# Three numbers that set the order of a mixer's instructions: the block inverse and the spatial gate are placed earlier

## The chip, the cores and the metric

The kernel runs on one NeuronCore of a Trainium2 chip. The time is that of the device in microseconds (us), from the start of the program to its end on that core. Engines are called as in the profile: PE (TensorE), DVE (VectorE), ACT (ScalarE), POOL (GpSimd) and SP (SyncE, which here only issues transfers).

## The reference

One encoder layer over S = 1024 frames of D = 1024 channels, in float32. What matters here:

```python
x = layer_norm(x)
proj = x @ w_in                               # u, v, r, k, val, wd, ad, gd, two gates
y_a = gelu(u) * (w_s @ layer_norm(gelu(v)) + b_s)      # spatial gate, blocks of 128 frames
for t in frames:                              # RWKV7: 16 heads of 64 channels
    sa    = state @ (-kk[t])
    state = state * w[t] + outer(sa, kk[t] * a[t]) + outer(v[t], k[t])
    y[t]  = state @ r[t]
y_b = (group_norm(y) + bonus) * g
m = sigmoid(gate_a) * y_a + sigmoid(gate_b) * y_b
x = layer_norm(alpha * x + m @ w_o)
x = layer_norm(alpha * x + conv_ffn(x))
```

## The kernel before

**Three parts.** The head makes the first layer norm and the spatial gate's normed v. The mixer makes everything up to the layer norm after w_o. The convolutional FFN ends the program. All wide products are of 128x512 with both operands split into two parts of reduced precision, so that one product takes three matmuls (`xh,wh`, `xlo,wh`, `xh,wl`, into `ps`). ACT casts a weight block to `wh`, and POOL subtracts to make `wl<-wr,wh`.

**Units.** The mixer's recurrence runs over 16 units: unit u is half h = u % 2 (512 frames, 8 chunks of 64) of the pair of heads p = u // 2. Each unit has four stages, named by letters in `run` (L1018):

- A, `stage_a` (L639), prepares unit u+2 while unit u runs: decays `gams`, normed keys (with a round trip through memory, SP's `q_d<-f`, `rc<-q_d`, `q_d<-rc`, `f<-q_d`), the products `ar<-tkr,gams` and `f<-f` on POOL, `bd<-f` and `ar<-f,gams` on DVE, the score products `pp<-ar,bd` on PE, which DVE masks into `ny<-pp,tri` and `ar<-pp,tri`; then four transfers `a_d<-ny` put 32x32 blocks to memory.
- B, `stage_b` (L732), inverts the triangular blocks of unit u+1: four transfers `bd<-a_d` bring them in one block to a partition; DVE copies `ydx<-rowm`; POOL runs 31 pairs of `tm<-ydx,bd` and `ydx<-ydx,tm`, each waiting for the one before; DVE transposes (`ydx<-ydx`, then four times `ny<-ydx`); PE multiplies `pp<-ydx,ny` and `pp<-ny,ydx`, with ACT copies between.
- C, `stage_chain` (L772), is the sequential pass over the 8 chunks (`pc`, `py`, `xs`, `bs`, `sgm`), which needs the inverse of its unit.
- F, `stage_fin`, ends a unit.

Around them stand the spatial gate Z (`stage_z`, L861: a small product with the mask, `bsb`, `fs<-pp,par,bsb` on DVE, two `gu<-gu,fs` on POOL) and the wide products U, W, X, k, r, v, which are only work to fill PE.

Buffers: `bd`, `ydx`, `tm` exist once; `ar`, `bs`, `ny` and the memory block `a_d` twice, by half. In the instruction lists `ar_1476`, `ny_1480`, `a_d_69` belong to even units and `ar_1477`, `ny_1481`, `a_d_70` to odd ones; `q_d_65` and `q_d_67` serve the norms of even units, `q_d_66` and `q_d_68` those of odd ones.

**What sets the order.** All instructions of the mixer are recorded by a class `Weave` first, with their dependencies and a modelled cost. `order` (L218) then lays them out by list scheduling over five queues (PE, DVE, ACT, POOL, SP): it takes the queue that can start something earliest, and of the instructions that can start there the one with the smallest `(o.prio, o.seq)` (L237). Its result is emitted as it stands (L279), so each engine runs a fixed list, and an instruction whose operand is late holds up all that follow it on its engine. `at(u, cls, ...)` (L999) gives a stage its priority, 100 * u + cls; with cls None the PE instructions go last of all (10^6 and up) and the others get 100 * u + 3. The whole mixer therefore shows as L279 in the profile, and the head and the FFN as L92.

Of the kernel before, what the change touches and what calls it, by code (L numbers as in the profile page):

```python
# [283 lines left out]
def hybrid_block(ctx: ExitStack, tc, x, w_in, w_v, pars, rows, bs, ws, lor, w_o, w_up, w_dn, out):  # L284
    nc = tc.nc
    W = Weave(tc)
# [296 lines left out]
    with ExitStack() as st:  # L583
# [415 lines left out]
        def at(u, cls, fn, *args):  # L999
            tick[0] += 1  # L1000
            n = 10 ** 6 + tick[0]
            W.prio = (lambda key: n if key == "T" else 100 * u + 3) if cls is None else 100 * u + cls
            W.cls = fn.__name__
            return fn(*args)
# [13 lines left out]
        def run(ch, u):  # L1018
            p, h = divmod(u, 2)
            if ch == "C":  # L1020
                at(u, 0, stage_chain, p, h)
            elif ch == "B" and u + 1 < NU:
                at(u, 10, stage_b, *divmod(u + 1, 2))
            elif ch == "A" and u + 2 < NU:
                at(u, 8, stage_a, *divmod(u + 2, 2))
            elif ch == "F":
                at(u, 5, stage_fin, p, h)
            elif ch == "v" and p + 1 < NPAIR:
                at(u, None, stage_g, p + 1, "v")
            elif ch in "kr" and p + 2 < NPAIR:  # L1030
                at(u, None, stage_g, p + 2, ch)
            elif ch in "UWZX":
                q = done[ch]
                if q < NPAIR - (ch in "XW") and (q < done["X"] + 1 and q < p + 1
                                                 if ch != "X" else ("yb", q, 1) in gen):
                    done[ch] += 1
                    at(u, 30 if ch == "Z" else None, {"U": stage_u, "W": stage_ga, "Z": stage_z, "X": stage_gb}[ch], q)

        done = dict.fromkeys("UWZX", 0)
        for u in range(NU - 1):  # L1040
            for ch in {0: "CFvUBAZW", 1: "CFBArXkW", NU - 3: "CFBAZW", NU - 2: "XUCFBZ"}.get(
                    u, "CFBAZWkr" if u % 2 else "XCFvUBA"):
                run(ch, u)
        u = NU - 1
# [196 lines left out]
```

## Time and profile before

| | |
|---|---|
| time, median of 3 runs (lowest to highest) | 1964.5 us (1964.23 to 1970.06) |
| time of the profiled execution | 1965.61 us |
| its span, first to last instruction | 1963.8 us |
| granted clock of TensorE, mean | 0.982 |
| PE busy | 1854.9 us, 94% |
| PE weight load (PEld) busy | 1499.5 us, 76% |
| DVE, ACT, POOL busy | 994.2, 857.2, 916.0 us |

PE is busy nearly all the time; PEld is the loading of weights into the array, which overlaps PE. A busy share is a mean over the head, the mixer (whose last wide product on PE starts at 1264.00 us) and the FFN.

### The profile page before, as it was taken

To read this page: it belongs to the slowest core of one execution; us is meant where nothing else is said; L and a number is where in the kernel's file an instruction comes from. 1 tells how busy PE (TensorE), PEld (TensorE's weight loads), DVE (VectorE), ACT (ScalarE), POOL (GpSimd) and SP (SyncE) were. 2 spreads that over 40 slices of the span, in tenths; PEclk is the share of its full clock that TensorE was granted. 3 is DMA by queue.
4 is the path that set the end of the run, shared out by engine and by line. 5 is a ranking of instruction groups with operands and counts; after the bars stand their busy time and mean duration, and the time that the engine had idled before them with its cause. 6 is when DMAs were issued, how large, how long until landed. Compare 5 with 4: busy or idle time off the path is not lost.

```text
span 1963.8 us, 27242 instructions
## 1 busy us (share of the span) xinstructions
PE 1854.9 (94%) x10024; PEld 1499.5 (76%) x10024; DVE 994.2 (51%) x1806; ACT 857.2 (44%) x1733; POOL 916.0 (47%) x1505
## 2 busy tenths in 40 slices
PE   6997899999999999999998899989999999999997
PEld 5996677677777777777776677768888888888886
DVE  8423745666555567555554467683333332333327
ACT  5544465655556566556565565421212121212121
POOL 5202575557656565675548662272423232323224
PEclk9998999999999999999998999999999999999999
DMA  6112121111112122112131322231111111111102
GB/s 211 33 49 61 46 64 58 52 46 47 55 52 68 55 54 63 38 58 65 47 93 55 97 86 62 79 115 44 54 43 55 42 55 42 57 41 58 39 1 86
DMA packets 78884, 119.13 MB, mean 61 GB/s; under 512 B 27776, under 2 KB 47488, under 8 KB 78752
## 3 DMA queue, kind: packets, MB, share of 16 engines
q1 hardware_dynamic: 60640, 96.94, 16.3%
q10 hardware_dynamic: 18112, 20.45, 3.2%
q8 instruction: 80, 1.31, 0.3%
q14 instruction: 52, 0.43, 0.1%
HBM read 103.08 MB, written 14.29 MB: 60 GB/s over the span
## 4 chain that ended last, share of the span: by engine, by line
PE 64%; POOL 17%; DVE 9%; issue 4%; ACT 3%; DMA 2%; ACTq 1%; POOLq 0%; SPq 0%; DVEq 0%
PE ps L279 17%; PE ps L92 11%; PE pu L92 11%; PE pd L92 10%; PE pp L279 8%; POOL ydx L279 6%; POOL tm L279 6%; PE pv L92 4%; PE pc L279 2%; POOL wl L279 2%; POOL ar L279 1%; PE py L279 1%; DVE ln_st L92 1%; DVE vl L92 1%; DVE f L92 1%
## 5 line engine op out<-in xcount | busy, mean ns | idle before, releaser
L279 PE MATMUL ps<-xh,wh 128*128 128x512 f32 x896 | 373.4, 417 | 33.2 <-DVE tkr L279 13.1
L279 PE MATMUL ps<-xh,wl 128*128 128x512 f32 x896 | 369.2, 413 | 6.6 <-POOL wl L279 6.3
L279 PE MATMUL ps<-xlo,wh 128*128 128x512 f32 x896 | 373.3, 417 | 0.0
L279 PEld LDWEIGHTS ps<-xh,wh 128*128 128x128 f32 x896 | 173.4, 194 | 66.3 <-DVE tkr L279 14.6
L279 PEld LDWEIGHTS ps<-xh,wl 128*128 128x128 f32 x896 | 173.0, 193 | 37.3 <-POOL wl L279 8.3
L279 POOL TENSOR_TENSOR tm<-ydx,bd 128x60 f32<-128x60 f32 (+24 forms) x496 | 167.3, 337 | 67.4 <-DMA bd<-a_d 12.4
L279 PEld LDWEIGHTS ps<-xlo,wh 128*128 128x128 f32 x896 | 173.2, 193 | 29.0 <-issue 1.0
L279 POOL TENSOR_TENSOR wl<-wr,wh 128x1024 fp32r<-128x1024 f32 x50 | 122.3, 2445 | 149.7 <-ACT wh L279 130.3
L92 DVE SCALAR_TENSOR_TENSOR t<-gb,par,t 128x512 f32<-128x512 f32 x84 | 89.6, 1067 | 193.4 <-ACT t L92 192.0
L279 POOL TENSOR_TENSOR ydx<-ydx,tm 128x60 f32<-128x60 f32 (+24 forms) x496 | 167.0, 337 | 37.2
L279 DVE SCALAR_TENSOR_TENSOR bs<-pc,gams,sgm 64x64 f32<-64x64 f32 x240 | 67.9, 283 | 161.5 <-PE pc L279 159.2
L92 POOL TENSOR_TENSOR fdl<-wr,fdh 128x1024 fp32r<-128x1024 f32 x21 | 51.4, 2463 | 196.4 <-ACT fdh L92 196.4
L92 PE MATMUL pd<-fdh,th 128*128 128x512 f32 x336 | 130.7, 389 | 0.0
L92 PE MATMUL pd<-fdl,th 128*128 128x512 f32 x336 | 130.7, 389 | 0.0
L92 PE MATMUL pd<-fdh,tl 128*128 128x512 f32 x336 | 130.7, 389 | 0.0
L92 ACT CAST fdh<-wr 128x1024 fp32r<-128x1024 f32 x21 | 21.5, 1051 | 196.5 <-PE pd L92 182.7
L92 POOL TENSOR_TENSOR wl<-wr,wh 128x1024 fp32r<-128x1024 f32 x22 | 56.3, 2560 | 63.6 <-ACT wh L92 63.6
L92 POOL TENSOR_TENSOR ful<-wr,fuh 128x1024 fp32r<-128x1024 f32 x20 | 48.7, 2437 | 78.7 <-ACT fuh L92 72.9
L279 PEld LDWEIGHTS pp<-ar,bd 64*128 64x128 f32 x512 | 61.8, 189 | 27.6 <-issue 17.8
L279 ACT ACTIVATE sgm<-bs,gams 128x128 f32<-128x128 f32 x128 | 51.4, 401 | 71.1 <-DVE bs L279 67.6
L92 POOL TENSOR_TENSOR tl<-t,th 128x512 fp32r<-128x512 f32 x42 | 55.6, 1325 | 56.2 <-DVE th L92 56.2
L279 PE MATMUL pp<-ar,bd 64*128 64x128 f32 x512 | 74.8, 288 | 6.1 <-DVE ar L279 4.7
(356 smaller groups left out, 4460.8 us busy)
## 6 DMA issues: line engine op xcount, KB each, us to landing
wr<-in_dram SPq DMA_DIRECT2D x113, 512.0 KB
bd<-a_d SPq DMA_DIRECT2D x64, 128.0 KB
vraw<-in_dram SPq DMA_DIRECT2D x8, 528.0 KB
xt<-in_dram SPq DMA_DIRECT2D x8, 512.0 KB
v_d<-xt ACTq DMA_DIRECT2D x8, 512.0 KB
fv<-v_d ACTq DMA_DIRECT2D x16, 256.0 KB
f<-q_d SPq DMA_DIRECT2D x32, 128.0 KB
m_d<-gu ACTq DMA_DIRECT2D x14, 256.0 KB
```

Source lines behind the costliest of these rows:

```text
L92: return fn(*a, **k)
L279: fn(*a, **k)
```

## The change

Two of the numbers in `run` change. B's class goes from 10 to 6, so that at one u the inverse of unit u+1 stands ahead of A, the preparation of unit u+2 (8). Z's goes from 30 to 4, ahead of F (5), B and A and behind the chain C (0) and the work of the wide products on engines other than PE (3). No instruction is added, removed or altered in shape; the five queues of the mixer get another order.

```diff
             if ch == "C":
                 at(u, 0, stage_chain, p, h)
             elif ch == "B" and u + 1 < NU:
-                at(u, 10, stage_b, *divmod(u + 1, 2))
+                at(u, 6, stage_b, *divmod(u + 1, 2))
             elif ch == "A" and u + 2 < NU:
                 at(u, 8, stage_a, *divmod(u + 2, 2))
             elif ch == "F":
...
-                    at(u, 30 if ch == "Z" else None, {"U": stage_u, "W": stage_ga, "Z": stage_z, "X": stage_gb}[ch], q)
+                    at(u, 4 if ch == "Z" else None, {"U": stage_u, "W": stage_ga, "Z": stage_z, "X": stage_gb}[ch], q)
```

On POOL, at the end of the inverse of unit 7 (the pairs of `tm` and `ydx`), there stood before:

```order
L279 TENSOR_TENSOR tm<-ydx,bd 128x35
L279 TENSOR_TENSOR ydx<-ydx,tm 128x7x5
L279 TENSOR_TENSOR ar_1476<-tkr,gams 64x8x64 x2
L279 TENSOR_TENSOR tm<-ydx,bd 128x28
L279 TENSOR_TENSOR ydx<-ydx,tm 128x7x4
...
L279 TENSOR_TENSOR tm<-ydx,bd 128x8
L279 TENSOR_TENSOR ydx<-ydx,tm 128x8
```

Of the change, the same place on POOL reads:

```order
L279 TENSOR_TENSOR tm<-ydx,bd 128x28
L279 TENSOR_TENSOR ydx<-ydx,tm 128x7x4
...
L279 TENSOR_TENSOR tm<-ydx,bd 128x8
L279 TENSOR_TENSOR ydx<-ydx,tm 128x8
L279 TENSOR_TENSOR ar_1476<-tkr,gams 64x8x64 x2
```

The two products `ar` of the preparation of unit 8 left the inverse and follow it.

On PE, at the end of the inverse of unit 6, before, the score products of unit 7 (`ar_1477,bd`) stood ahead of the product that takes up the inverse of unit 6 (`ydx,ny_1480`):

```order
L279 MATMUL pp<-ar_1477,bd 128x128 x4
L279 MATMUL ps<-xh_119,wh 128x512
L279 MATMUL pp<-ident,bd 128x128 x4
...
L279 MATMUL pp<-cm,tv 128x128 x3
L279 MATMUL pp<-f,bones 128x512
...
L279 MATMUL pp<-ydx,ny_1480 32x32 x16
L279 MATMUL ps<-xh_119,wh 128x512
```

Of the change they stand behind it:

```order
L279 MATMUL pp<-ident,ff 128x128 x4
L279 MATMUL pp<-gd_136,g0w 128x512
L279 MATMUL pp<-gd_137,g1w 128x512
L279 MATMUL pp<-ydx,ny_1480 32x32 x16
L279 MATMUL pp<-ar_1477,bd 128x128
L279 MATMUL ps<-xh_119,wh 128x512
L279 MATMUL pp<-ar_1477,bd 128x128 x3
L279 MATMUL pp<-ny_1480,ydx 32x32
```

The preparation of the next unit and the end of the inverse changed places.

On SP, the four loads `bd<-a_d_70` of unit 7 and the round trip of the norms of unit 8 (`q_d_65`, `rc`, `q_d_67`), before:

```order
L279 DMA a_d_70<-ny_1481 32x8x32 x2
L279 DMA bd<-a_d_70 32x1024 x2
L279 DMA q_d_65<-f 1x512
L279 DMA lraw<-in_dram 128x384
L279 DMA bd<-a_d_70 32x1024
L279 DMA q_d_65<-f 1x512
L279 DMA rc<-q_d_65 128x8
L279 DMA bd<-a_d_70 32x1024
L279 DMA wr<-in_dram 128x1024
L279 DMA q_d_67<-rc 128x8
L279 DMA f<-q_d_67 64x512 x2
```

Of the change:

```order
L279 DMA a_d_70<-ny_1481 32x8x32
L279 DMA q_d_65<-f 1x512
L279 DMA bd<-a_d_70 32x1024
L279 DMA rc<-q_d_65 128x8
L279 DMA bd<-a_d_70 32x1024
L279 DMA q_d_67<-rc 128x8
L279 DMA wr<-in_dram 128x1024
L279 DMA bd<-a_d_70 32x1024
L279 DMA f<-q_d_67 64x512 x2
L279 DMA bd<-a_d_70 32x1024
```

The fourth load, without which the inverse can't start, moved behind the whole round trip of the next unit's norms.

## Rows read from the trace of the kernel before

**Rows 1.** The page: busy time of each engine, share of the span, instructions.

```profile
PE 1854.9 (94%) x10024; PEld 1499.5 (76%) x10024; DVE 994.2 (51%) x1806; ACT 857.2 (44%) x1733; POOL 916.0 (47%) x1505
```

**Rows 2.** The page: the chain that ended last, share of the span by engine.

```profile
PE 64%; POOL 17%; DVE 9%; issue 4%; ACT 3%; DMA 2%; ACTq 1%; POOLq 0%; SPq 0%; DVEq 0%
```

**Rows 3.** Windows, inverse 2 to 14: us, busy PE PEld DVE ACT POOL, clock, DMA.

```profile
602.20:712.50 110.30, 108.92 (x699) 84.07 (x700) 67.00 (x143) 67.92 (x158) 73.52 (x154) 1.00 0.19 56
...
952.50:1091.30 138.80, 125.55 (x756) 97.62 (x752) 70.11 (x146) 77.23 (x167) 82.15 (x158) 0.96 0.25 78
sum 724.50, PE 690.50 PEld 535.92 DVE 415.08 ACT 425.05 POOL 440.67; mean PE 115.08 PEld 89.32 DVE 69.18 ACT 70.84 POOL 73.44
```

**Rows 4.** Windows behind them: the mixer's end, and the FFN.

```profile
1091.30:1200.00 108.70, 99.16 (x601) 76.98 (x601) 63.47 (x123) 66.34 (x157) 72.55 (x104) 0.95 0.26 82
1200.00:1964.00 764.00, 743.77 (x3287) 614.54 (x3285) 314.55 (x439) 182.23 (x273) 247.29 (x149) 0.99 0.17 54
```

**Rows 5.** The page, costliest groups: POOL's weight split: busy, mean ns, idle before.

```profile
L279 POOL TENSOR_TENSOR wl<-wr,wh 128x1024 fp32r<-128x1024 f32 x50 | 122.3, 2445 | 149.7 <-ACT wh L279 130.3
```

**Rows 6.** Timelines, POOL (inverse 6) and one DVE row, 553 to 597 us: start, us, instruction.

```profile
555.82 1.26 POOL L279 TENSOR_TENSOR gu<-gu,fs 128x512 f32<-128x512 f32 x1 [0.33 <-DVE fs L279]
...
562.19 0.24 POOL L279 TENSOR_TENSOR tm<-ydx,bd 128x31 f32<-128x31 f32 x1 [4.90 <-DMA bd<-a_d]
...
579.71 2.45 POOL L279 TENSOR_TENSOR ar<-tkr,gams 64x512 f32<-64x512 f32 x2
...
586.84 0.31 POOL L279 TENSOR_TENSOR ydx<-ydx,tm 128x60 f32<-128x60 f32 x1
...
586.92 1.50 DVE L279 TENSOR_TENSOR bd<-f 64x512 f32<-64x512 f32 x2
...
587.94 0.64 POOL L279 TENSOR_TENSOR ydx<-ydx,tm 128x66 f32<-128x66 f32 x1
...
595.83 0.21 POOL L279 TENSOR_TENSOR ydx<-ydx,tm 128x8 f32<-128x8 f32 x1
```

**Rows 7.** POOL's timeline, 1100 to 1128 us: first and last step of unit 15's inverse.

```profile
1103.05 0.24 POOL L279 TENSOR_TENSOR tm<-ydx,bd 128x31 f32<-128x31 f32 x1
...
1127.11 0.21 POOL L279 TENSOR_TENSOR ydx<-ydx,tm 128x8 f32<-128x8 f32 x1
```

**Rows 8.** POOL's and DVE's timelines, 342 to 366 us (end of unit 2's inverse).

```profile
343.92 3.23 POOL L279 TENSOR_TENSOR ar<-tkr,gams 64x512 f32<-64x512 f32 x2
...
349.04 1.27 POOL L279 TENSOR_TENSOR f<-f 128x512 f32<-128x512 f32 x1
...
360.86 0.21 POOL L279 TENSOR_TENSOR ydx<-ydx,tm 128x8 f32<-128x8 f32 x1
...
364.49 0.43 DVE L279 STREAM_TRANSPOSE ydx<-ydx 128x256 f32<-128x256 f32 x1
```

**Rows 9.** PE's timeline, 538 to 548 us: last score products of 6, first product behind inverse 5.

```profile
539.99 0.79 PE L279 MATMUL pp<-ar,bd 64*128 64x128 f32 x2
...
547.01 0.69 PE L279 MATMUL pp<-ydx,ny 32*32 32x32 f32 x32
```

**Rows 10.** SP's timeline, 536 to 620 us: transfers as they are issued (units 6, 7).

```profile
559.70 0.45 SPq L279 DMA_DIRECT2D bd<-a_d  x1
...
611.28 0.45 SPq L279 DMA_DIRECT2D bd<-a_d  x1
...
618.43 1.11 SPq L279 DMA_DIRECT2D f<-q_d  x2
```

**Rows 11.** POOL's, DVE's and PE's timelines, 1060 to 1092 us (end of unit 14's inverse).

```profile
1061.71 0.21 POOL L279 TENSOR_TENSOR ydx<-ydx,tm 128x8 f32<-128x8 f32 x1
...
1087.20 0.43 DVE L279 STREAM_TRANSPOSE ydx<-ydx 128x256 f32<-128x256 f32 x1
...
1091.33 0.69 PE L279 MATMUL pp<-ydx,ny 32*32 32x32 f32 x32
```

**Rows 12.** The chain that ended last, 1380 to 1400 us: start, length, instructions.

```profile
1386.86 10.88 PE pu L92 x48
```

## The prediction

> **What bounds the kernel now.** I read the page's busy times first: PE is busy 94% of the span and no other engine more than 51% [rows 1]. The chain that ended last is PE for 64%, POOL for 17% and DVE for 9% [rows 2], so for a good part of the mixer POOL's inverse and what stands round it set the end. Then I cut the mixer into pairs of units, from the first product behind the inverse of one even unit to that of the next, units 2 to 14 [rows 3]. Six pairs take 724.5 us with PE busy 690.5 of them, so 34.0 are idle. The fastest pair takes 110.3, the last 138.8, and the first five (724.5 - 138.8) / 5 = 117.1 on average. Behind these PE idles 108.70 - 99.16 = 9.5 us (the rest of the recurrence) and 764.00 - 743.77 = 20.2 us (almost all FFN) [rows 4]. The change adds no work, so all it can win or lose is idle time of PE, and stretches at the lower granted clock that follow such idle time (0.96 in the pair of 138.8, 1.00 in the fastest).
>
> **What the order is worth in PE's time.** Two prices: a wide matmul 10.88 / 48 = 0.227 us [rows 12]; for the other rows of PE's list (small products, transposes) I take the fastest pair, whose list holds 264 wide and 173 others, so (110.3 - 264 x 0.227) / 173 = 0.29. Counted in the two lists, 2205 wide matmuls stood ahead of the inverse product of unit 14, and 2116 do now: 89 fewer, and some 31 others. That is 20.2 + 9.0 = 29 us of work moved behind unit 14. About half of it leaves the stretch ahead of unit 2 (26 wide, 31 others with the score products: 15 us), so the six pairs keep 690.5 - 14 = 676, or 112.7 a pair. From list counts (273 wide and 173 others) it is 112.1; I take 112.3 as the least that a pair can cost.
>
> **The change part by part.**
>
> *POOL inside the inverse.* Unit 15's inverse, which nothing interrupts, takes 1127.11 + 0.21 - 1103.05 = 24.3 us [rows 7]; unit 6's takes 595.83 + 0.21 - 562.19 = 33.9 [rows 6]. What stands between the steps explains it: `ar` x2, 2.45 [rows 6], `f`, 1.27 [rows 8], two weight splits `wl` at 2.445 [rows 5], and slowed steps. In the new list `ar` and `f` come behind the last step, and in even units the two `gu` (1.26 each [rows 6]), which ran ahead of the inverse before, partly enter it. In the lists an odd unit keeps one `wl`, an even one two `wl` and a `gu`: 24.3 + 2.4 = 26.7 and 24.3 + 4.9 + 1.3 = 30.5.
>
> One cost is not settled by the counts. A step takes 0.31 us and then 0.64 while DVE multiplies `bd<-f`, both operands of which lie in SBUF [rows 6]. The Trainium skill, "SBUF — State Buffer", section "Who interferes with whom", says that such a DVE instruction shares a read port with GpSimd and one of the two waits; the trace agrees. By that rule alone odd inverses would be about 1 us shorter, as the preparation moves behind them, some 6 us in all if the inverse were the path throughout; without it nothing changes in the sum below.
>
> *Behind the inverse.* In unit 2 the last step ends at 361.07 and the transposes start at 364.49, since DVE first masks the scores of unit 3 [rows 8]. In unit 14 the inverse ends at 1061.92, the transposes start at 1087.20 and the product at 1091.33 [rows 11]: 29.4 us, in which DVE's list stood at the preparation of unit 15, whose scores PE had not made. In the new list the transposes follow the inverse in both places, and the product about 2 us behind it (five transposes at 0.43 [rows 8], without a queue).
>
> *What this pushes back.* Before, the last score products of unit 6 came at 539.99 + 0.79 = 540.8, 6.2 us ahead of the product behind the inverse of unit 5 [rows 9]. Now they come behind it: in odd units after 6 wide matmuls, 16 score products and the small ones, 7 us; in even units after some 46 wide and 19 others, 10.4 + 5.5 = 16 us. So everything that hangs on the scores (the four `a_d` stores, the four `bd` loads, the inverse) starts later against the inverse before. From the last score product to the first inverse step it took 562.19 - 540.8 = 21.4 us in unit 6 [rows 6, 9].
>
> *SP.* The last `bd` load of unit 7 was issued at 611.28 and the round trip of the next norms ended with `f<-q_d` at 618.43 + 1.11 = 619.54 [rows 10]. In the new list this load stands behind `f<-q_d`: at the worst 8.3 us later, at the best nothing, if the round trip is over by the time the scores are stored. In unit 6 the load came 559.70 - 540.8 = 18.9 us behind the scores, and the inverse 2.5 us behind the load [rows 6, 10]. With the earlier load in odd units (unit 7's scores came at 597.5, so 13.8 + 2.5 = 16.3 [rows 10]) the bounds for scores to inverse are 16.3 and 21.4; I take 18.5, near their middle, since unit 6 already had the load behind `q_d<-rc` and odd units now get the same.
>
> *The sum for a pair.* The new path runs from one inverse to the next: odd 7 + 18.5 + 26.7 + 2 = 54.2, even 16 + 18.5 + 30.5 + 2 = 67.0, together 121.2. That is an upper bound in so far as each link is on the path with its full length; PE's own work, 112.3, is the lower one. The middle is 116.8, which I take: hardly less than the 117.1 of the first five pairs, and much less than the last one's 138.8.
>
> *Sum over the program.* (1) Up to unit 2's product: `ar` 3.23 and `f` 1.27 leave the inverse, the wait of 3.4 us ahead of the transposes goes, and some 1.4 of PE's queue: -9.3. (2) Six pairs: 6 x 116.8 - 724.5 = -23.7. Nearly all of it is the last pair. (3) The 29.2 us of PE work that are now owed behind unit 14, less 5 that fit into half of the 9.5 us of idle time there: +24.2. Together -8.8. The profiled execution took 1965.6 us with a span of 1963.8; the median of the runs is 1.1 lower. 1965.6 - 8.8 - 1.1 = 1955.7, say **1956 us**.
>
> Of Z alone I count nothing apart: the two `gu`, ready 6 us ahead of the inverse before [rows 6], are needed by the wide products' followers much later; what they cost is the 1.3 us in even inverses.
>
> **The rivals.**
>
> *R1, slower: the preparation becomes the path.* For it speaks that all slack between the inverse and its product goes to the scores, that SP's last load stands behind the next unit's round trip, and that a unit's late product holds up the fixed list of PE. Against it, that PE has 112.3 us of work in a pair to put in between. With pairs at 121.2 to 122 the sum is -9.3 + 2.7 (or 7.5) + 24.2 = +18 to +22: **1982 to 1987 us**. It decides where a pair takes more than (724.5 + 9.3 - 24.2) / 6 = 118.3, which is 1.5 us over my own value.
>
> *R2, a larger gain: PE's idle time goes.* With pairs at 112.3 the sum is -9.3 - 50.7 + 24.2 = -35.8: **1929 us**. For it speaks the fastest pair, 110.3 at clock 1.00. Against it, the path of 121.2. By the Trainium skill, "Perfetto Trace Analysis", section "Identifying the Most-Contended Engine", matmul busy time says little of the distance to the best, and the share of weight loading says more. It was 535.92 / 724.5 = 74.0% in the pairs and 614.54 / 764 = 80.4% in the FFN; the trace so leaves some 58 us of room in the pairs, if they could be as dense as the FFN, which the small products speak against.
>
> *R3, no change.* PE is busy 95% of the pairs; its list holds the same work, and what one stretch wins the next owes (term 3 alone gives back 24 of 33). That the chance waits of the last pair only move to another place also belongs here. **1964 us**, within 3.
>
> **How the numbers follow.** My case 0.38 (pairs from 115 to 118.5, that is 1945 to 1966), R1 0.27, R2 0.20, R3 0.15. Of my case two thirds lie over 0.3% (6 us) faster, the rest within 0.3%; 0.3% is also about what a measurement of this kernel can tell. Faster 0.20 + 0.26 = 0.46; within 0.3% 0.12 + 0.11 = 0.23; slower 0.27 and the rest of R3 = 0.31. The range takes in R2's 1930 and R1's 1988.
>
> **What would show it.** In POOL's timeline: inverses of 26 to 31 us with `ar` and `f` behind them. In DVE's: transposes within 1 us of the last step, in unit 14 too. In PE's: the product behind an inverse within 3 us of its end, and the scores of the next unit 7 (odd) or 16 us (even) behind it. Pairs of about 117 us, the last one too, and about 24 us more between unit 14's product and the FFN. The prediction is wrong if pairs exceed 118.3, which would show as PE waiting for DVE's `ydx` or for ACT's copies in the inverse, with POOL waiting for `bd<-a_d` before it; or if the stretch behind unit 14 doesn't grow.

## The result and the profile after

The change made the kernel slower: 2068.93 us median of 4 runs (2068.61 to 2069.32), against 1966.32 us (1964.23 to 1970.06), a ratio of 1.0522 with a 95% interval of 1.0509 to 1.0535. (The 1964.5 us ahead of the prediction are the median of three of these four runs of the kernel before.) The forecast was 1956, at most 1988.

The page of the changed kernel, busy times and the chain that ended last, by engine; both answer to [rows 1, 2]:

```profile
PE 1909.8 (92%) x10024; PEld 1549.4 (75%) x10024; DVE 984.8 (48%) x1806; ACT 853.7 (41%) x1731; POOL 902.8 (44%) x1505
...
PE 65%; POOL 18%; DVE 9%; issue 5%; ACT 2%; DMA 1%; ACTq 0%; SPq 0%; POOLq 0%; DVEq 0%
```

The span grew from 1963.8 to 2067.3 us, 103.5. PE was busy 54.9 us longer with the same 10024 matmuls, and idle 48.6 us longer. So the loss has two halves: PE stands, and PE works more slowly.

Windows of the changed kernel between the same products as in [rows 3] (unit 2's at 364.7, unit 14's at 1167.5) and behind them as in [rows 4]; columns as there:

```profile
899.20:1034.20 135.00, 125.44 (x720) 97.63 (x720) 65.83 (x141) 69.41 (x160) 70.33 (x157) 0.90 0.16 48
1034.20:1167.50 133.30, 119.22 (x699) 92.61 (x701) 68.40 (x143) 72.76 (x163) 68.99 (x156) 0.90 0.19 55
sum 802.80, PE 727.43 PEld 568.03 DVE 400.95 ACT 421.60 POOL 418.09; mean PE 121.24 PEld 94.67 DVE 66.83 ACT 70.27 POOL 69.68
```

```profile
1167.50:1303.00 135.50, 129.13 (x741) 104.08 (x742) 75.48 (x140) 75.00 (x172) 87.75 (x113) 0.93 0.30 94
1303.00:2067.00 764.00, 742.72 (x3286) 613.68 (x3284) 314.06 (x439) 182.01 (x273) 247.07 (x149) 0.99 0.17 54
```

The six pairs take 802.8 us instead of 724.5, that is 133.8 each. The FFN is what it was. Idle time in the pairs rose from 34.0 to 75.4. Busy time rose from 690.5 to 727.4 although, by the lists, 63 wide matmuls fewer stand in this stretch (14.3 us at 0.227): 727.4 - (690.5 - 14.3) = some 51 us are, by this estimate, the price of a granted clock of 0.90 instead of 0.98.

Two waits of the changed kernel that grew (total, times, longest), PE's from 150 to 1400 us and DVE's from 360 to 1170:

```profile
PE pp L279 <- DVE ydx L279: 82.0, 15, 10.1
```

```profile
DVE ydx L279 <- POOL ydx L279: 85.7, 13, 11.8
```

The same rows in the kernel before:

```profile
PE pp L279 <- DVE ydx L279: 7.5, 3, 4.0
DVE ydx L279 <- POOL ydx L279: 6.0, 1, 6.0
```

DVE's one wait of before was at the inverse of unit 15, behind the six pairs. Read together: DVE now stands at the transposes for POOL's last step, 85.7 us instead of 6.0, and PE stands at the product for DVE's transposes, 82.0 us instead of 7.5. One such place, the end of unit 7's inverse, in the timelines of the changed kernel (POOL, then DVE, then PE):

```profile
688.73 0.21 POOL L279 TENSOR_TENSOR ydx<-ydx,tm 128x8 f32<-128x8 f32 x1
688.89 2.77 POOL L279 TENSOR_TENSOR ar<-tkr,gams 64x512 f32<-64x512 f32 x2
...
688.97 0.45 DVE L279 STREAM_TRANSPOSE ydx<-ydx 128x256 f32<-128x256 f32 x1 [4.30 <-POOL ydx L279]
...
693.62 2.08 DVE L279 SCALAR_TENSOR_TENSOR f<-f 128x512 f32<-128x512 f32 x2
...
701.04 2.98 DVE L279 TENSOR_TENSOR bd<-f 64x512 f32<-64x512 f32 x3
703.94 0.69 DVE L279 TENSOR_TENSOR ar<-f,gams 64x512 f32<-64x512 f32 x1
...
684.96 0.39 PE L279 MATMUL ps<-xlo,wh 128*128 128x512 f32 x1
689.56 1.06 PE L279 MATMUL pp<-ydx,ny 32*32 32x32 f32 x32 [4.21 <-DVE ydx L279]
...
691.58 0.63 PE L279 MATMUL ps<-xlo,wh 128*128 128x512 f32 x1
...
702.82 1.38 PE L279 MATMUL pp<-ar,bd 64*128 64x128 f32 x10
...
708.29 1.16 PE L279 MATMUL pp<-ar,bd 64*128 64x128 f32 x8
```

The transposes do follow the inverse at once. But behind them in DVE's list stands the preparation of unit 8 (`f<-f`, `bd<-f`, `ar<-f,gams`), which needs nothing of the inverse. As far as the timelines show, the last operand of the two `f<-f` and the first `bd<-f` was made at 684.48 on ACT, so these 2.76 us of work could have run in the 4.30 us before. The next `bd<-f` came later for another reason: it needs ACT's `f<-f,oka,hpar`, and ACT had stood 6.70 us at its copy of the inverse's second product with this instruction behind it. POOL's `ar`, too, stands behind the last step. So the last scores of unit 8 are ready at 708.29 + 1.16 = 709.45, 20.5 us behind the inverse of unit 7, and unit 8's stores, loads and inverse can't start before. That inverse gates the next preparation in the same way: the two stages that ran side by side now run in turn. (PE itself never stood from the product to these scores: it had the fill work that its list put ahead of them.)

Windows round the same place show what the 4.21 us of waiting did to PE (columns as in [rows 3]; the last but two is the granted clock):

```profile
684.00:689.50 5.50, 1.35 (x6) 0.77 (x5) 1.17 (x3) 1.99 (x3) 4.40 (x16) 0.94 0.00 1
689.50:695.40 5.90, 5.84 (x43) 4.77 (x44) 5.72 (x8) 0.73 (x2) 5.69 (x5) 0.50 0.12 44
695.40:702.80 7.40, 7.40 (x62) 5.49 (x60) 4.11 (x6) 3.03 (x7) 2.18 (x4) 0.98 0.27 74
```

After the wait PE works 5.9 us at a granted clock of 0.50, the lower of its two levels, and then at full speed again. The Trainium skill, "TensorE: Matmul & The Clock Gate", Part 1, says that the gate follows how busy PE has just been and halves the clock; here the trace agrees. This is the mild case. One unit earlier PE stood 7.33 us, and the clock stayed at 0.50 for 17.7 us (626.76 to 644.50) in which PE never stood; its list there is mostly small products, the scores of unit 7 among them:

```profile
626.76 1.06 PE L279 MATMUL pp<-ydx,ny 32*32 32x32 f32 x32 [7.33 <-DVE ydx L279]
627.76 0.79 PE L279 MATMUL pp<-ar,bd 64*128 64x128 f32 x2
```

### The profile page after: what moved, and what is told of

It is laid out like the page before. It is cut to its first block, busy times and chain, and to the rows that moved or that the text cites. A ratio compares the mean times of both kernels' runs of the same rounds, so it can differ in the third digit from the quotient of the medians.

```text
span 2067.3 us, 27216 instructions
## 1 busy us (share of the span) xinstructions
PE 1909.8 (92%) x10024; PEld 1549.4 (75%) x10024; DVE 984.8 (48%) x1806; ACT 853.7 (41%) x1731; POOL 902.8 (44%) x1505
## 4 chain that ended last, share of the span: by engine, by line
PE 65%; POOL 18%; DVE 9%; issue 5%; ACT 2%; DMA 1%; ACTq 0%; SPq 0%; POOLq 0%; DVEq 0%
PE ps L279 17%; PE ps L92 10%; PE pp L279 10%; PE pu L92 10%; PE pd L92 10%; POOL ydx L279 8%; POOL tm L279 7%; PE pv L92 4%; PE pc L279 3%; POOL wl L279 3%; PE py L279 1%; DVE ln_st L92 1%; POOL gu L279 1%; DVE vl L92 1%; DVE f L92 1%
## 5 line engine op out<-in xcount | busy, mean ns | idle before, releaser
L279 PE MATMUL ps<-xh,wh 128*128 128x512 f32 x896 | 378.8, 423 | 17.6 <-ACT wh L279 10.5
L279 PE MATMUL ps<-xh,wl 128*128 128x512 f32 x896 | 378.5, 423 | 4.4 <-POOL wl L279 4.3
L279 PEld LDWEIGHTS ps<-xlo,wh 128*128 128x128 f32 x896 | 176.0, 196 | 30.5 <-issue 1.8
L92 ACT CAST fdh<-wr 128x1024 fp32r<-128x1024 f32 x21 | 21.4, 1049 | 196.2 <-PE pd L92 182.7
L279 PE MATMUL pp<-ar,bd 64*128 64x128 f32 x512 | 100.2, 357 | 0.0
L279 PEld LDWEIGHTS pp<-ar,bd 64*128 64x128 f32 x512 | 82.0, 247 | 21.3 <-issue 18.7
L279 PE MATMUL pp<-ydx,ny 32*32 32x32 f32 x512 | 15.9, 227 | 82.0 <-DVE ydx L279 82.0
L279 ACT COPY ny<-pp 64x256 f32<-64x256 f32 (+1 forms) x96 | 35.0, 365 | 119.5 <-PE pp L279 100.6
```

Source lines behind the costliest of these rows:

```text
L92: return fn(*a, **k)
L279: fn(*a, **k)
```

## The experiments

Two theories were named first. **Theory one, slack:** the planner takes an uninterrupted inverse for 17.7 us (62 steps at its modelled cost; the planner's figures are its own sums and no times of the chip), the trace has 24.3 [rows 7]; its plan before left 7 to 17 us between an inverse and its product, which covered the error, and the plan of the change leaves 1 us. **Theory two, the loop:** the order itself puts scores, stores, loads and inverse of one unit behind the inverse of the unit before. Each run stands against the kernel before on the same chip. Every edit gives the planner another problem, so all five lists change with it; a run tests the edit together with its new lists.

### Each number alone

The title speaks of three numbers; the change sets two, B's and Z's. B alone, against the change:

```diff
-                    at(u, 4 if ch == "Z" else None, {"U": stage_u, "W": stage_ga, "Z": stage_z, "X": stage_gb}[ch], q)
+                    at(u, 30 if ch == "Z" else None, {"U": stage_u, "W": stage_ga, "Z": stage_z, "X": stage_gb}[ch], q)
```

> B at 6, Z back at 30. Theory one (the planner takes an uninterrupted inverse for 17.7 us where the trace has 24.3; before, its plan left 7 to 17 us between the end of an inverse and the product that takes it up, which covered that; with B ahead of A the plan leaves 1 us, so PE stands ahead of each such product and then works at the lower clock): B alone does it, 2045 to 2075 us, PE waits over 60 us for ydx, pairs of 128 to 136 us. Rival (the gate's two products gu on POOL, now inside the even inverses, lengthen the path): B alone stays within 1% of before, 1950 to 1985.

Measured: 2084.59 us, 1.0593 (1.0577 to 1.0609), more than expected; pairs of 137.7, PE's wait for `ydx` 71.4 us.

Z alone, against the change:

```diff
-                at(u, 6, stage_b, *divmod(u + 1, 2))
+                at(u, 10, stage_b, *divmod(u + 1, 2))
```

> Z at 4, B back at 10. Theory one: the plan of this list keeps 5 to 19 us behind most inverses but only about 1 behind some, so PE's wait for ydx is a fraction of the 82 us of the change (10 to 35 us) and the time 1960 to 2000. Rival (the gate): most of the 103 us, 2030 or more.

Measured: 1974.82 us, 1.0033 (1.0020 to 1.0047), PE's wait for `ydx` 18.1 us. B does the damage; Z alone costs 0.3%, and beside B it takes away a part of the loss (2084.59 against 2068.93).

### The right cost of a step

```diff
-        return (... else 190 + 2.12 * n if n > 256 else 190 + 1.9 * n), 80
+        return (... else 190 + 2.12 * n if n > 256 else 297 + 1.9 * n), 80
```

> Both numbers as in the change, and the planner's cost of a small POOL product raised by 107 ns, so that it plans 24.3 us for an uninterrupted inverse. Theory one: the plan puts other work of PE ahead of the inverse's product again; PE's wait for ydx falls from 82 to under 25 us, the granted clock of the pairs rises from 0.90 to over 0.96, pairs of 110 to 119 us, time 1940 to 1985. Rival (path: the scores now stand behind the inverse's product, and the chain product, scores, stores, loads, inverse is longer than PE's work whatever the plan believes): pairs stay at 121 us or more, time 2000 to 2060, and PE waits as before at another instruction of that chain.

Measured with both numbers of the change: 2025.98 us, 1.0296 (1.0281 to 1.0312); pairs of 128.6, clock 0.90, PE's wait for `ydx` 42.6 us. Theory one had the sign and missed the size. The loop keeps pairs over 121.

> The numbers of before (B 10, Z 30) with the same raised cost. Theory one: the plan of before already had enough slack, so little is won: 1945 to 1985. If the raised cost by itself is what helps (a better plan whatever the numbers), it comes out below before by as much as the kernel with both numbers and the raised cost does. If the raised cost makes a plan that is worse (its slack behind the inverse grows where the slack was enough), 1985 to 2010.

Measured with the numbers of before: 1949.70 us, 0.9910 (0.9889 to 0.9932), faster than both kernels and inside theory one's range. The raised cost won 0.9% with these numbers and 43 us with those of the change; it doesn't cure B.

### Slack without the cost

```diff
             x1 = ydx[:, 1, :].rearrange("p (c t) -> p c t", t=32)
+            W.late = 12000
             V.transpose(x1.rearrange("p c (i q) -> p i c q", q=4), yd)
...
                 V.transpose(y3[QD[b], :, b // 2, ...], x1[QD[b]])
+            W.late = 0
```

> Both numbers as in the change; the planner is told that what the inverse's transposes write is ready 12 us later, so that it puts 12 us of other work of PE ahead of the inverse's product; nothing on the chip waits for that. Theory one: PE's wait for ydx under 15 us, clock as before, time 1945 to 1985. Theory two: the waits move to another link, pairs of 121 us or more, 2000 or more.

Measured: 2063.61 us, 1.0490 (1.0461 to 1.0518). The product no longer waits, others do. PE's waits in this run:

```profile
PE pp L279 <- POOL ar L279: 33.4, 6, 7.0
PE pp L279 <- DVE ff L279: 20.3, 7, 5.9
```

The first is the wait for the preparation's `ar` behind the inverse. Giving the slack back takes 5.3 us off the change, and the pairs stay at 135.6. So theory one falls as the whole cause, with one reserve: the new lists also moved the scores of even units, from 18.6 to 24.1 us behind the inverse before. The run with POOL's order alone, below, has no such reserve.

### The transfers' cost as well

```diff
-            return 60, 2000 + aps[0].size() * 4 / 150
+            return 450, 2000 + aps[0].size() * 4 / 150
```

> As the change with the step of the inverse planned at its measured length, and each transfer that SP issues planned at 450 ns on its queue (the trace: 0.45) instead of 60. The plan itself then has pairs of 114 us, longer than the 107 of PE's work in it: with these costs the planner sees the loop as the bound. Theory one: less waiting than with the step's cost alone, 1960 to 2015. Theory two: pairs of 121 us or more, and a time at or over the 2026 of the step's cost alone.

Measured: 2062.01 us, 1.0486 (1.0469 to 1.0503), pairs of 132.9, PE's wait for `ydx` 84.5 us. The planner told the truth about steps and transfers makes a regular loop, and no shorter one.

### Which engine's order

B's priority 6 on some engines only, 10 on the others, Z at 4:

```diff
-                at(u, 6, stage_b, *divmod(u + 1, 2))
+                at(u, lambda key: 6 if key in "G" else 10, stage_b, *divmod(u + 1, 2))
```

"G" is POOL; "V" (DVE), "GV", "TAS" (PE, ACT, SP) and "TGAS" (all but DVE) are the other runs.

> Z at 4; B at 6 on POOL alone, at 10 on PE, DVE, ACT and SP. The products ar of the next preparation stand behind the inverse on POOL, as in the change; the planned slack behind the inverses is 10 to 21 us. Theory one (slack): PE's wait for ydx stays under 15 us, time 1950 to 1985. Theory two (the loop: an inverse, then ar on POOL, then scores, stores, loads, the next inverse, which POOL's order closes): the loop is as in the change, pairs of 121 us or more, time 2010 to 2070.

Measured: 2018.88 us, 1.0267 (1.0250 to 1.0284). An instance at the end of unit 7's inverse, from this run's POOL and PE:

```profile
667.78 0.65 POOL L279 TENSOR_TENSOR ydx<-ydx,tm 128x8 f32<-128x8 f32 x1
668.38 1.61 POOL L279 TENSOR_TENSOR ar<-tkr,gams 64x512 f32<-64x512 f32 x1
...
670.05 1.51 PE L279 MATMUL pp<-ar,bd 64*128 64x128 f32 x10 [1.64 <-POOL ar L279]
...
686.05 0.69 PE L279 MATMUL pp<-ydx,ny 32*32 32x32 f32 x32
```

The scores wait for `ar`, which waits for the inverse, while the product comes 17.6 us behind the inverse, with slack to spare. In all, PE waits 40.1 us for `ar`: theory two's loop, nearly without theory one's symptom (6.7 us for `ydx`).

> Z at 4; B at 6 on DVE alone (the transposes behind an inverse go ahead of the preparation's masks), at 10 on all other engines, so ar may run inside the inverse on POOL. The planned slack is 1 to 4 us. Theory one: PE stands ahead of most of the products for ydx, 40 to 80 us in all, clock of the pairs 0.90 to 0.94, time 2000 to 2060. Theory two: no closed loop, within 1% of the kernel with Z alone (1955 to 1995).

Measured: 2001.59 us, 1.0186 (1.0162 to 1.0211). Neither expectation is met as put. The time lies at the edge of theory one's range, but PE's wait for `ydx` is 28.2 us, less than it asks; and theory two had left out that DVE's order by itself can hold the preparation back.

> Z at 4; B at 6 on POOL and DVE, at 10 on PE, ACT and SP. POOL alone cost 2.7% and DVE alone 1.9%, the whole change 5.2%. Loop theory (POOL puts the next preparation's ar, and DVE its masks, behind the inverse, so scores, stores, loads and the next inverse follow in series): the two together carry the whole loss, 2045 to 2085 us, pairs of 130 us or more. Rival (PE's own order, the inverse's product ahead of the scores, carries a part): 2000 to 2035.

Measured: 2070.35 us, 1.0532 (1.0510 to 1.0555): the whole loss.

> Z at 4; B at 6 on PE, ACT and SP, at 10 on POOL and DVE, the complement of the run with POOL and DVE. Loop theory: within 1% of Z alone (1975), so 1955 to 1995. Rival (PE's order carries a part): 2005 to 2050.

Measured: 1977.46 us, 1.0044 (1.0026 to 1.0062): what Z alone costs. So the order of POOL and DVE is the carrier, and that of PE, ACT and SP is not.

### POOL's product on the other engine

```diff
-                G.tensor_tensor(ar[rs, :, 3 - hd, :], c8(r)[rs], gam[rs, :, 1:65], ALU.mult)
+                V.tensor_tensor(ar[rs, :, 3 - hd, :], c8(r)[rs], gam[rs, :, 1:65], ALU.mult)
```

> The change, with the preparation's two products ar<-tkr,gams issued on DVE instead of POOL; the same numbers are computed. Loop theory: POOL's link (2.45 us a unit, and the place behind the inverse) leaves the loop, so pairs get at least 5 us shorter, 121 to 130, and the time is 1985 to 2045. Rival (POOL's ar is not in the loop, PE only waits there because it comes last): no change within 0.5%, 2058 to 2080.

Measured: 2054.50 us, 1.0449 (1.0433 to 1.0465), neither range. POOL's link is out, but DVE stands 56.5 us for POOL's `ydx` with the preparation behind it, so the loop stays closed there. Two more runs make two by two of it:

> Z at 4; B at 6 on PE, POOL, ACT and SP, at 10 on DVE; ar stays on POOL. Of two by two (ar on POOL or DVE; B ahead on DVE or not) this is ar on POOL, B not ahead on DVE. If either engine alone can hold the scores back behind an inverse, POOL does it here as in the run with POOL alone (2019): 2000 to 2040. If DVE's order is the carrier and POOL's only follows, 1960 to 1995.

Measured: 2037.89 us, 1.0349 (1.0327 to 1.0370).

> The same with ar issued on DVE: neither POOL's ar nor DVE's preparation stands behind the inverse. If the scores' wait on these two engines is the whole loss, the time is within 1% of Z alone (1975): 1950 to 1995, and the last score products come at most 12 us behind the inverse before, on average. If another product of POOL (f<-f) or PE's order carries a part, 2000 or more.

Measured: 1978.52 us, 1.0050 (1.0033 to 1.0068). The last scores come 12.2 us behind the inverse before on average (units 3 to 13), where 12 at most was expected.

| median, us | B ahead on DVE | B not ahead on DVE |
|---|---|---|
| `ar` on POOL, behind the inverse | 2068.93 | 2037.89 |
| `ar` on DVE | 2054.50 | 1978.52 |

Either engine alone closes the loop; only with both opened the loss falls to 0.5%, about what Z alone costs, though B still stands ahead on PE, POOL, ACT and SP.

### A kernel that beats both

B back at 10, Z at 4, the step's cost raised; then the transfers' cost as well.

> B at 10 as before, Z at 4, and the raised cost of the inverse's step. Z alone cost 0.3%, the raised cost alone won 0.9%. Loop theory: Z is not in the loop, its two gu only sit on POOL ahead of or in the inverse; with the right cost the time is within 1% of the kernel with the raised cost alone, 1935 to 1970. Rival (Z's place by itself costs slack): 1970 to 1995.

Measured: 1935.15 us, 0.9842 (0.9823 to 0.9860).

> The best kernel so far (B 10, Z 4, raised cost of the inverse's step: 1935) with SP's issue planned at 450 ns as well. PE's work is the bound there, so a better plan of SP can win little: 1925 to 1945; if the planned slack of 1 us behind even inverses is too small, 1945 to 1965.

Measured: 1927.51 us, 0.9789 (0.9769 to 0.9809). With the planner's two costs so, B at 6 took 2062.01 (above): 134.5 us more. A window over its six pairs, columns as in [rows 3], and the inverse of unit 7 on POOL with the scores of unit 8 on PE:

```profile
375.00:1052.30 677.30, 668.28 (x4246) 521.92 (x4246) 421.26 (x844) 428.00 (x964) 441.83 (x930) 1.00 0.20 60
```

```profile
611.80 0.24 POOL L279 TENSOR_TENSOR tm<-ydx,bd 128x31 f32<-128x31 f32 x1 [3.07 <-DMA bd<-a_d]
...
631.55 1.20 POOL L279 TENSOR_TENSOR ar<-tkr,gams 64x512 f32<-64x512 f32 x1 [1.03 <-ACT gams L279]
633.41 1.20 POOL L279 TENSOR_TENSOR ar<-tkr,gams 64x512 f32<-64x512 f32 x1
...
648.45 0.21 POOL L279 TENSOR_TENSOR ydx<-ydx,tm 128x8 f32<-128x8 f32 x1
...
646.55 1.16 PE L279 MATMUL pp<-ar,bd 64*128 64x128 f32 x8
```

The preparation's `ar` interrupts the inverse, which takes 36.9 us and not 26.7 as in the change, and the last scores of unit 8 are made 0.9 us before it ends. PE is busy 668.28 of 677.30 us at clock 1.00, and a pair takes 112.9. The longer inverse goes with the shorter pair here, since the next preparation runs inside it.

## Why the prediction was wrong

**Term 1, up to unit 2's product (-9.3): measured 364.7 - 366.8 = -2.1.** The inverse did get shorter and the transposes did follow it. From its first step to the product it took 27.7 us instead of 37.0, which is the 9.3 put in. But its first step came at 337.0 instead of 329.8: the start was not in the sum.

**Term 2, six pairs (-23.7): measured 802.8 - 724.5 = +78.3. This is the term that failed**, in two steps. Of the 17.0 us that a pair took over the forecast (133.8 - 116.8), the first is 4.4 and the second 12.6.

The first is the choice in "the sum for a pair". R1's path was there, 121.2 us, and I took 116.8, the middle between it and PE's own 112.3. A loop that runs through every unit isn't averaged with the work beside it: the longer of the two decides. R1 was the right rival and should have been the forecast; with its 121.2 the time would have come out near 1982, still 87 us short.

The second is the size of the path. Its links, worked out from the timelines as means over units 3 to 13, with what I had put in:

| link, us | odd: put in | odd: measured | even: put in | even: measured |
|---|---|---|---|---|
| inverse before to last scores | 2 + 7 = 9 | 14.2 | 2 + 16 = 18 | 18.6 |
| last scores to inverse | 18.5 | 22.1 | 18.5 | 20.0 |
| inverse | 26.7 | 27.0 | 30.5 | 31.7 |
| sum | 54.2 | 63.3 | 67.0 | 70.3 |

Together 133.6, against 133.8 by the windows. That agreement proves nothing: the links follow each other without a gap, from the end of one inverse to the end of the next, so they must add up to a pair. What the table shows is where the time lies. In the kernel before the same links were 2.2, 18.9 and 32.6 for odd units, 10.1, 20.5 and 33.0 for even ones, in sum 117.3. So the inverses lost 6.9 us a pair, nearly as the lists had promised (steps slowed beside DVE's work stayed: in unit 7's inverse a `ydx` took 0.65 us at 680.18, during DVE's `ff<-ff,bvs`), and the way to the scores gained 20.5.

Most of that gain had been put in. The table is 12.4 over the 121.2, and the largest parts are the odd way to the scores (5.2) and the odd way from there to the inverse (3.6).

*The odd way to the scores.* The prediction priced it from PE's list, and the list was read rightly: the first score products ran about 1.0 us behind the inverse's product in five of six odd units, and between that product and the last scores PE was busy for 171.59 of 171.61 us in units 3 to 13. What was wrong was the clock. In the same five units the stretch ran at 0.50, the lower level, and the six took 13.6 us on average where 7 stood in the sum. Unit 7's and unit 8's (columns as in [rows 3]):

```profile
626.76:639.71 12.95, 12.95 (x101) 9.67 (x101) 5.99 (x12) 4.31 (x10) 4.37 (x8) 0.50 0.04 6
689.56:709.45 19.89, 19.89 (x144) 15.41 (x144) 14.90 (x21) 6.62 (x15) 7.99 (x9) 0.85 0.16 44
```

An estimate from these windows, each length times its clock: at full clock the odd way would have taken 7.4 and the even one 14.1 instead of 13.6 and 18.0. So the lower clock lengthened the path by some 10 us a pair, and without it the path would have been near 123.5, close to R1's 121.2. The wait for the inverse slows the very work on which the next inverse hangs.

*The odd way from the scores to the inverse.* In all six odd units the last `bd` load was issued right behind the round trip's `f<-q_d`, 17.7 us behind the scores on average, against 14.6 before, and the first step came 4.5 us behind the load instead of 2.5. The link came out over the upper of the two bounds, 16.3 and 21.4, between which the 18.5 was taken. From unit 7, whose scores were made at 639.7:

```profile
656.65 1.16 SPq L279 DMA_DIRECT2D f<-q_d  x2
657.86 0.59 SPq L279 DMA_DIRECT2D bd<-a_d  x1
```

The step of the prediction that failed is so "the sum for a pair": it let PE's work shorten a path that PE's work can't shorten, and it added up that path at full clock. "Behind the inverse" had the transposes and the product right (the product 0.6 us behind the inverse), and "What this pushes back" followed PE's and SP's lists from there; neither followed DVE's list, which now stands at the transposes until POOL is done, with the next preparation behind. By the runs with the order of a few engines each and Z at 4 throughout (0.3% by itself), B ahead on PE, ACT and SP comes to 0.4%, on POOL to 2.7%, on DVE to 1.9%, on POOL and DVE to 5.3%.

**The clock was left out.** The prediction's opening names the stretches at the lower clock that follow idle time; no term had them. They are some 51 us of the 103.5, over the kernel before, which had some of them too (0.96 in its last pair).

**Term 3, work owed behind unit 14 (+24.2): measured 899.8 - 872.5 = +27.3.** Right, to 3.1 us.

**R2** (112.3 a pair) was within reach, by other means: 112.9 with B at 10 and right costs. There the share of weight loading in the pairs is 521.92 / 677.30 = 77.1%, up from 74.0%. By "Identifying the Most-Contended Engine" of the Trainium skill's "Perfetto Trace Analysis" this share shows the room left; between these two kernels it rose with the gain. It did not in the change with the step's right cost: 586.48 / 771.80 = 76.0% there, more than the 74.0% of before, in longer pairs, because the loads themselves took 586.48 us instead of 535.92, at a clock of 0.90 instead of 0.98. A share that grows because the loads grow longer is no gain:

```profile
364.90:1136.70 771.80, 731.11 (x4278) 586.48 (x4280) 417.22 (x854) 414.46 (x958) 426.61 (x933) 0.90 0.18 52
```

**What stays open.** The planner's raised cost took 43 us off the change in one run and, with the transfers' cost beside it, gave nearly all of it back; why the one list is that much better than the other was not followed up. The share of the clock in the loss and in the path is worked out from the windows, not taken away by an experiment.

## What to carry to other kernels

When a list is fixed and each engine runs it in order, ask of every instruction that moves forward what stands behind it while it waits: a stage that waits for a long serial one must not stand ahead of work that needs nothing from it. When stages of successive units form a loop, forecast the loop's whole length, not a middle between it and the busiest engine's work, and price the work in it at the clock that the waits leave it. And correct the planner's costs from the trace before its priorities are tuned: 24.3 us for 17.7 won 0.9% alone, and the same Z that cost 0.3% before won 0.7% on top of it.

## What the runs showed of the hardware

A wait of PE is paid for twice here. After 4.21 us of standing the next 5.9 us ran at a granted clock of 0.50; after 7.33 us the next 17.7 did, mostly small products, with PE busy throughout. Over the pairs the slower work (51 us) cost more than the added standing (75.4 - 34.0 = 41.4 us).
